# Hybrid streaming encoder step, `down` of the MLP: the order of two products, one tile pool for `up` and `down`, and the queue that loads x

## The chip, the cores and the metric

The kernel runs on one core of one Trainium2 chip. The time is that of one execution on the device, in microseconds (us); three runs of the kernel before the change took 2486.47, 2488.69 and 2491.09 us. A core has five engines that matter here: TensorE (PE in the profile; PEld is its weight load), VectorE (DVE), ScalarE (ACT), GpSimd (POOL) and SyncE (SP). Each runs its own instructions in order and waits for the others by semaphores. Transfers between DRAM and on-chip memory are issued by SP (the hardware queue q1 in the profile) and by POOL (the software queue q0), and both are served by the same 16 DMA engines.

## What is computed

One step of a two-layer encoder over T = 1024 + 64 frames of width 1024. Layer 0 mixes frames by windowed attention, layer 1 by a gated recurrence, and each layer ends in an MLP:

```python
def sqrelu_mlp(h, w_up, w_down):
    return jnp.square(jax.nn.relu(h @ w_up)) @ w_down
...
        yp = yp + sqrelu_mlp(rmsnorm(yp, mlp_norm[i]), mlp_w_up[i], mlp_w_down[i])
        ys = ys + sqrelu_mlp(rmsnorm(ys, mlp_norm[i]), mlp_w_up[i], mlp_w_down[i])
```

`w_up` is 1024 x 4096 and `w_down` 4096 x 1024, in fp32. The results are y of all frames, and the new caches and states of the mixers.

## The kernel before

**Numbers.** Every operand of TensorE is split into a rounded part and the rest (`hi` and `lo`, tiles `eh`/`el`, `xh`/`xl`, `whi`/`wlo`). A product then takes three matmuls: hi by hi, lo by hi, hi by lo. The rounding is a cast on ScalarE, the rest a subtraction on VectorE (lines 117 and 118 for weights, 998 and 999 for the operands of `down`).

**Products.** `up` and `down` each multiply a 2 x 2 block matrix by a 2 x 2 block matrix in seven products of sums of blocks. For `down` the table `PRODS` (from line 31) has a row for each: the weight blocks that are added or subtracted, the name of the operand, where the result is added in x, and the four slots that hold the operand. A slot is two tiles next to each other: `x2` is xh[2], xl[2], xh[3] and xl[3], so a product's operand has eight pieces of 128 x 1088.

**From `up` to `down`.** `up` runs over 16 pairs m of output blocks. At the end of each it holds four results (y) and forms five sums of them on VectorE (tiles `d1` or `d`, line 903). All are written to DRAM by POOL's queue (`keep`, line 840, tensor `y_mlp`), by the row of `PRODS` that uses them; piece k of an operand needs pairs 2k and 2k + 1. The last piece, number 7, needs the last pair. While `up` works x lies in DRAM (`x_mlp`), and its tiles `pair0` to `pair3` are `up`'s work space.

**`down`.** For product j, for each of four pairs m of output blocks, and for each slot i: `weights` loads a 256 KB block through SP's queue (line 1003, tile `raw`), loads a second one and adds or subtracts it where the row of `PRODS` has two (line 1010, tile `q`), and splits it; `mul` (line 1021) then issues 4 x 2 x 3 = 24 matmuls of 128 x 272. The result lies in one of four accumulators (`pu`), and `evacuate` (line 1030) adds it to x. As soon as an operand tile is read for the last time in product j, `load(j + 1, i)` (line 997) brings the next piece through POOL's queue. In product 0 the x tiles are loaded again, too (lines 1093 and 1095). At the end of layer 1 `normed` (line 1046) writes y.

**Tiles and their waits.** A tile comes from a pool. A pool that is opened after another was closed lies in the same memory, and its first tiles wait for all that the closed pool's tiles still do, their transfers included. Within a pool a tag has a fixed number of buffers, and a buffer is used again when its last reader is done. Before the change `up` has a pool `up` (tags `tt`, `d1`, `raw`, `q`) that closes before the pool `down` (`raw`, `q`, `y`) opens. The first weight block of a sum goes to a third pool that lives throughout (`raw`, three buffers); so do the split weights, two tiles of two halves each.

**What sets the order.** The program is written as above, but a scheduler orders each engine's instructions by a simulated time line, so instructions of `down` stand among the last of `up`.

Of the kernel before, what the change touches and what calls it, by code (L numbers as in the profile page):

```python
# [8 lines left out]
F32 = mybir.dt.float32  # L9
# [6 lines left out]
PSUM = bass.MemoryType.PSUM  # L16

P = 128
# [10 lines left out]


PRODS = (
# [18 lines left out]
class Trunk:  # L50
# [933 lines left out]
    def down(self, layer, final, hp, acc):  # L984
        nc, tc, A = self.nc, self.tc, self.A
        self.CH = CH4

        def pair_of(slot):
            i = int(slot[1])
            return [(self.eh, self.el) if slot[0] == "e" else (self.xh, self.xl)][0], (i, i + 1)  # L990


        def load(j, i):
            (hs, ls), n = pair_of(PRODS[j][3][i])
            for q, k in enumerate(n):
                y = ls[k][:].bitcast(F32)
                nc.gpsimd.dma_start(y, self.yk[layer][j, 2 * i + q].rearrange("p a n -> p (a n)"))
                nc.scalar.copy(hs[k][:], y)
                nc.vector.tensor_sub(ls[k][:], y, hs[k][:].bitcast(F32))

        def raw(m, block, i, own):
            r = self.raw() if own else hp.tile([P, 4, P], F32, name="raw", tag="raw", bufs=3)
            nc.sync.dma_start(r[:], A["w_down"][layer, 2 * m + block[0], :, block[1], 4 * i:4 * i + 4, :])
            return r[:]

        def weights(a, m, i):
            r = raw(m, a[0], i, True)
            if len(a) > 1:
                q = hp.tile([P, 4, P], F32, name="q", tag="q", bufs=2)[:]
                nc.vector.tensor_tensor(q, r, raw(m, a[2], i, False), ALU.add if a[1] == "+" else ALU.subtract)  # L1010
                r = q
            return self.parts(r)

        def mul(ps, w, j, i, cs, first, last):
            (hs, ls), n = pair_of(PRODS[j][3][i])
            for k in range(4):
                t, o = n[k // 2], TH * (k % 2)
                for c in cs:
                    s = slice(o + TH // 2 * c, o + TH // 2 * c + TH // 2)
                    for x, (a, b) in enumerate(((0, hs), (0, ls), (1, hs))):  # L1020
                        done = nc.tensor.matmul(ps[:, c, :], w[k][a], b[t][:, s], start=first and k == x == 0,  # L1021
                                                stop=last and k == 3 and x == 2)
            return done

        def evacuate(ps, m, outs, cs=(0, 1)):
            n = TH // 2
            for r, h, f in outs:
                for t, u in [(self.xp[m][:, r, TH * h:TH * h + TH].rearrange("p (c n) -> p c n", c=2), ps)] \
                        if len(cs) == 2 else [(self.xp[m][:, r, TH * h + n * c:TH * h + n * c + n], ps[:, c, :]) for c in cs]:
                    nc.vector.tensor_tensor(t, t, u, ALU.add if f == "+" else ALU.subtract)  # L1030

        def scale(k, cs):
            if not final:
                for c in cs:
                    self.scale_part(2, k, c)

        def square(k, cs):
            for c in cs:
                done = self.square_part(k, c)
            return done  # L1040

        def normed(c, ks):
            s, n = self.CH[c]
            for k in ks:
                y = hp.tile([P, 272], F32, name="y", tag="y", bufs=6)
                nc.vector.scalar_tensor_tensor(y[:, :n], self.x(k)[:, s:s + n], self.gains[:, 4, k:k + 1],
                                               self.rstd[:, s:s + n], ALU.mult, ALU.mult)
                nc.sync.dma_start(self.O["y"][:, k, s:s + n], y[:, :n])

        def norm(c):  # L1050
            self.norm_scale(c, acc()[:, 0, :])

        H0, H1 = (0, 1), (2, 3)
        self.xp = [None] * 4
        for i in range(4):
            load(0, i)
        done = None
        for j, (a, name, outs, slots) in enumerate(PRODS):
            end = j == len(PRODS) - 1
            for m in range(4):  # L1060
                order = list(range(4))
                if m == 3:
                    i = 3 if end else slots.index(PRODS[j + 1][3][3])
                    order = [i] + [k for k in order if k != i]
                ps = acc()
                if end and final and m == 3:
                    self.half = None
                    w = {i: weights(a, m, i) for i in order}
                    for c in range(2):
                        for i in order:  # L1070
                            mul(ps, w[i], j, i, (c,), i == order[0], i == order[-1])
                        evacuate(ps, m, outs, (c,))
                        done = square(7, (2 + c,))
                        if c == 0:
                            norm(2)
                            normed(2, range(3))
                    norm(3)
                    with tc.issue_after(done.ins):
                        normed(2, range(3, KT))
                        normed(3, range(KT))  # L1080
                    return
                for i in order:
                    last = mul(ps, weights(a, m, i), j, i, (0, 1), i == order[0], i == order[-1])
                    if end and m == 3 and i == order[0]:
                        for k in (0, 1):
                            scale(k, H0)
                        scale(0, H1)
                        scale(1, H1)
                if j == 0:
                    self.xp[m] = self.pair(m)  # L1090
                    if done:
                        with tc.issue_after(done.ins):
                            nc.sync.dma_start(self.xp[m][:], self.xk[layer][:, 2 * m:2 * m + 2, :])
                    else:
                        nc.sync.dma_start(self.xp[m][:], self.xk[layer][:, 2 * m:2 * m + 2, :])
                done = last
                evacuate(ps, m, outs)
                if not end and m < 3:
                    load(j + 1, m)

                if j == 5:
                    square(2 * m, H1)
                if end:
                    square(2 * m + 1, H1)
                    if m in (1, 2):
                        scale(2 * m + 1, H1)
                    if final and m < 2:
                        norm(m)
                        normed(m, range(KT))
            if not end:  # L1110
                load(j + 1, 3)
            if j == 4:
                self.new_norm()
                for k in range(KT):
                    square(k, H0)
            if j == 5:
                for k in range(2, KT):
                    scale(k, H0)
                for k in (2, 4, 6):
                    scale(k, H1)  # L1120
        scale(7, H1)

    def mlp(self, layer, wa, wb, na, final):
        tc = self.tc
        with ExitStack() as ctx:
            ep = ctx.enter_context(tc.tile_pool(name=f"mlp{layer}", bufs=1))
            with ExitStack() as c2:
                up = c2.enter_context(tc.tile_pool(name=f"up{layer}", bufs=1))
                with ExitStack() as c3:
                    self.banks(c3, f"mr{layer}", 8)  # L1130
                    op = self.operands(1 + 2 * layer, ep, up)
                    self.mix_rest(wa, wb, op, na)
                pu = ctx.enter_context(tc.tile_pool(name=f"pu{layer}", bufs=4, space=PSUM))

                def acc():
                    return pu.tile([P, 2, 512], F32, name="pu", tag="pu")[:, :, :TH // 2]

                self.up(layer, op, up, acc)
            with ExitStack() as c2:
                hp = c2.enter_context(tc.tile_pool(name=f"down{layer}", bufs=1))  # L1140
                self.down(layer, final, hp, acc)

    def run(self):
        A = self.A
# [131 lines left out]
```

## Time and profile before

| | |
|---|---|
| median of three runs | 2488.69 us |
| the profiled execution | 2486.93 us |
| its span, first to last instruction | 2485.2 us |
| mean granted TensorE clock | 0.984 of full speed |
| traffic of DRAM | 252.80 MB read, 81.79 MB written |
| hardware queue (SP) | 205.96 MB, 25.9% of the 16 engines' span |
| software queue (POOL) | 135.26 MB, 14.4% |

The profile is of one execution. An engine's busy time is the sum of its instructions; time in which it stands is put down to what released it. In layer 0 `up` ends and `down` begins at about 738 us of the span, in layer 1 at about 2099 us. A timeline row has the start, the length, the engine, the line, the operation and, in brackets, the idle time before it and its releaser. A row of waits has the engine and tile that waited, what for, the total, how often and the longest.

### The profile page before, as it was taken

Reading aid. Unit: us, or ns where it says so; the run is one execution under the profiler, and the core shown is the slowest. Engines: PE = TensorE matmul, PEld = TensorE weight load, DVE = VectorE, ACT = ScalarE, POOL = GpSimd, SP = SyncE. Lnnn points to the kernel's source line nnn. Section 1 sums busy time; section 2 is a strip of 40 time slices with the busy share of each in tenths; the row PEclk is TensorE's granted clock in tenths of the full one; section 3 lists DMA queues with packets and bytes.
Section 4 is the critical chain, followed back from the end, with each engine's and each line's share of the span. In section 5 each row is a group of like instructions: output and inputs, shape, how many; then the busy total and the mean of one; then the engine's idle time right before and its main releaser. Section 6 shows DMA issues by size and latency. Waiting matters only on the chain.

```text
span 2485.2 us, 46519 instructions
## 1 busy us (share of the span) xinstructions
PE 2389.9 (96%) x18474; PEld 2334.2 (94%) x18474; DVE 1747.8 (70%) x3120; ACT 1079.4 (43%) x2200; POOL 238.9 (10%) x481
## 2 busy tenths in 40 slices
PE   8999999999986999999999999999999997799997
PEld 7998899999986999999999999998999997799997
DVE  7555559877775577677677777776987777557766
ACT  5236546333342433445455555554633334243342
POOL 2211100111120100000000000000011113000000
PEclk9999999999998999999999999999999999899999
DMA  5322123443367687561111011023244446667764
GB/s 168 85 56 68 38 89 112 149 146 142 142 232 243 215 276 250 185 214 35 38 38 37 30 38 38 25 91 117 96 145 147 142 146 261 224 226 264 242 197 152
DMA packets 158922, 344.20 MB, mean 139 GB/s; under 512 B 35296, under 2 KB 47200, under 8 KB 154976
## 3 DMA queue, kind: packets, MB, share of 16 engines
q1 hardware_dynamic: 120784, 205.96, 25.9%
q0 software_dynamic: 37920, 135.26, 14.4%
q8 instruction: 146, 2.39, 0.4%
q14 instruction: 72, 0.59, 0.1%
HBM read 252.80 MB, written 81.79 MB: 135 GB/s over the span
## 4 chain that ended last, share of the span: by engine, by line
PE 73%; issue 17%; DMA 4%; POOL 3%; DVE 2%; ACT 1%; POOLq 0%; SPq 0%; DVEq 0%; ACTq 0%
PE pu L1021 18%; PE pu L891 13%; PE mm L127 10%; PE mm L129 9%; PE mm L128 9%; POOL y_mlp L840 2%; PE sc L341 2%; PE po L375 2%; PE pb L651 2%; PE pu L878 1%; DMA xl<-y_mlp 1%; DMA y_mlp<-d 1%; DMA raw<-in_w_down 1%; PE pb L615 1%; PE pt L369 1%
## 5 line engine op out<-in xcount | busy, mean ns | idle before, releaser
L127 PE MATMUL mm<-xh,whi 128*128 128x384 f32 (+2 forms) x1440 | 478.9, 333 | 13.9 <-ACT whi L117 11.7
L128 PE MATMUL mm<-xl,whi 128*128 128x384 f32 (+2 forms) x1440 | 474.7, 330 | 0.0
L129 PE MATMUL mm<-xh,wlo 128*128 128x384 f32 (+2 forms) x1440 | 473.5, 330 | 0.0
L1021 PE MATMUL pu<-xh,wlo 128*128 128x272 f32 x1024 | 296.4, 289 | 0.5 <-DVE wlo L118 0.3
L1021 PE MATMUL pu<-xh,whi 128*128 128x272 f32 x1024 | 296.0, 289 | 0.5 <-DVE pair L1030 0.5
L1021 PE MATMUL pu<-xl,whi 128*128 128x272 f32 x1024 | 295.7, 289 | 0.0
L127 PEld LDWEIGHTS mm<-xh,whi 128*128 128x128 f32 x1440 | 272.3, 189 | 19.7 <-ACT whi L117 12.8
L117 ACT CAST whi<-raw 128x512 fp32r<-128x512 f32 (+1 forms) x288 | 166.4, 608 | 261.6 <-PE mm L128 92.0
L1021 PE MATMUL pu<-eh,whi 128*128 128x272 f32 x768 | 224.3, 292 | 56.4 <-ACT whi L117 56.4
L891 PE MATMUL pu<-xh,wlo 128*128 128x272 f32 x960 | 276.6, 288 | 0.0
L128 PEld LDWEIGHTS mm<-xl,whi 128*128 128x128 f32 x1440 | 272.5, 189 | 3.5 <-issue 2.2
L891 PE MATMUL pu<-xl,whi 128*128 128x272 f32 x960 | 275.6, 287 | 0.0
L891 PE MATMUL pu<-xh,whi 128*128 128x272 f32 x960 | 275.4, 287 | 0.0
L129 PEld LDWEIGHTS mm<-xh,wlo 128*128 128x128 f32 x1440 | 272.2, 189 | 3.1 <-issue 1.2
L117 ACT CAST whi<-q 128x512 fp32r<-128x512 f32 x220 | 130.6, 618 | 279.7 <-PE pu L1021 187.6
L118 DVE TENSOR_TENSOR wlo<-raw,whi 128x512 fp32r<-128x512 f32 (+1 forms) x288 | 187.5, 673 | 62.4 <-ACT whi L117 61.9
L118 DVE TENSOR_TENSOR wlo<-q,whi 128x512 fp32r<-128x512 f32 x220 | 146.3, 687 | 112.1 <-ACT whi L117 111.5
L1021 PE MATMUL pu<-eh,wlo 128*128 128x272 f32 x768 | 224.0, 292 | 0.1
L1021 PE MATMUL pu<-el,whi 128*128 128x272 f32 x768 | 223.5, 291 | 0.0
L891 PE MATMUL pu<-eh,wlo 128*128 128x272 f32 x720 | 208.0, 289 | 0.0
L891 PE MATMUL pu<-eh,whi 128*128 128x272 f32 x720 | 207.5, 288 | 0.0
L891 PE MATMUL pu<-el,whi 128*128 128x272 f32 x720 | 207.0, 287 | 0.0
(281 smaller groups left out, 5529.0 us busy)
## 6 DMA issues: line engine op xcount, KB each, us to landing
raw<-in_w_down SPq DMA_DIRECT2D x384, 256.0 KB, 3.8
y_mlp<-d POOLq DMA_DIRECT2D x160, 272.0 KB, 2.5
xl<-y_mlp POOLq DMA_DIRECT2D x64, 544.0 KB, 8.0
raw<-in_w_up SPq DMA_DIRECT2D x128, 256.0 KB, 2.7
el<-y_mlp POOLq DMA_DIRECT2D x48, 544.0 KB, 6.9
y_mlp<-pair POOLq DMA_DIRECT2D x64, 272.0 KB, 2.4
raw<-in_w_in SPq DMA_DIRECT2D x64, 256.0 KB, 2.9
x_mlp<-pair SPq DMA_DIRECT2D x8, 1088.0 KB, 4.9
```

The lines of the kernel that those rows point to most:

```text
L117: nc.scalar.copy(hi, raw)
L118: nc.vector.tensor_sub(lo, raw, hi.bitcast(F32))
L127: nc.tensor.matmul(ps[:, :n], wh, ih[:, s:s + n], start=i == 0, stop=False)
L128: nc.tensor.matmul(ps[:, :n], wh, il[:, s:s + n], start=False, stop=False)
L129: nc.tensor.matmul(ps[:, :n], wl, ih[:, s:s + n], start=False, stop=i == last)
L341: nc.tensor.matmul(ps[u][:, i, :kn], st, kd[g][r, k0:k0 + kn], start=True, stop=True)
L369: nc.tensor.transpose(pt[:, kt, :], pb[:, u, kt * P:(kt + 1) * P], self.ident[:])
L375: nc.tensor.matmul(out, ptts[u][:, kt, :], v, start=start, stop=stop)
L651: nc.tensor.matmul(psa[r:r + 64 - hh, i // 2, :].rearrange("p (s t) -> p s t", t=hh), d[:, i * 64:i * 64 + 64 - hh], dv[:, i * ns:(i + 1) ...
L840: self.nc.gpsimd.dma_start(self.yk[layer][i, p // 2, :, p % 2, :], t)
L891: nc.tensor.matmul(ps[:, c, :], a, cols(b)[:, c, :], start=not more and p == i == 0, stop=p == 3 and i == 2, skip_group_check=True)
L1021: done = nc.tensor.matmul(ps[:, c, :], w[k][a], b[t][:, s], start=first and k == x == 0, stop=last and k == 3 and x == 2)
```

## The change

The first two rows of `PRODS` change places, but the slots stay with the place: product 0 is now the one of a single weight block, with the operand b21-b11, and product 1 the one of a sum, with b11. `up` and `down` share one pool, open from `up`'s start to `down`'s end; the second block of a sum has two buffers in it where it had three, and the y of the last norm is put into the tags `tt` and `d1`. The x tiles of product 0 are loaded through POOL's queue in place of SP's.

```diff
--- before.py
+++ after.py
@@ -29,8 +29,8 @@
 
 
 PRODS = (
-    (((1, 0), "+", (1, 1)), "b11", ((1, 0, "+"), (1, 1, "-")), ("e0", "e2", "x0", "x2")),
-    (((1, 1),), "b21-b11", ((1, 0, "+"), (0, 0, "+")), ("e4", "x4", "x6", "x0")),
+    (((1, 1),), "b21-b11", ((1, 0, "+"), (0, 0, "+")), ("e0", "e2", "x0", "x2")),
+    (((1, 0), "+", (1, 1)), "b11", ((1, 0, "+"), (1, 1, "-")), ("e4", "x4", "x6", "x0")),
     (((0, 1), "-", (1, 1)), "b21+b22", ((0, 0, "+"),), ("e0", "e2", "x2", "x4")),
     (((0, 0), "+", (0, 1)), "b22", ((0, 0, "-"), (0, 1, "+")), ("e4", "x0", "x6", "x2")),
     (((0, 0), "+", (1, 1)), "b11+b22", ((0, 0, "+"), (1, 1, "+")), ("e0", "e2", "x4", "e4")),
@@ -999,7 +999,7 @@
                 nc.vector.tensor_sub(ls[k][:], y, hs[k][:].bitcast(F32))
 
         def raw(m, block, i, own):
-            r = self.raw() if own else hp.tile([P, 4, P], F32, name="raw", tag="raw", bufs=3)
+            r = self.raw() if own else hp.tile([P, 4, P], F32, name="raw", tag="raw", bufs=2)
             nc.sync.dma_start(r[:], A["w_down"][layer, 2 * m + block[0], :, block[1], 4 * i:4 * i + 4, :])
             return r[:]
 
@@ -1042,7 +1042,7 @@
         def normed(c, ks):
             s, n = self.CH[c]
             for k in ks:
-                y = hp.tile([P, 272], F32, name="y", tag="y", bufs=6)
+                y = hp.tile([P, TH], F32, name="y", tag=("tt", "d1")[k % 2], bufs=3 + k % 2)
                 nc.vector.scalar_tensor_tensor(y[:, :n], self.x(k)[:, s:s + n], self.gains[:, 4, k:k + 1],
                                                self.rstd[:, s:s + n], ALU.mult, ALU.mult)
                 nc.sync.dma_start(self.O["y"][:, k, s:s + n], y[:, :n])
@@ -1090,9 +1090,9 @@
                     self.xp[m] = self.pair(m)
                     if done:
                         with tc.issue_after(done.ins):
-                            nc.sync.dma_start(self.xp[m][:], self.xk[layer][:, 2 * m:2 * m + 2, :])
+                            nc.gpsimd.dma_start(self.xp[m][:], self.xk[layer][:, 2 * m:2 * m + 2, :])
                     else:
-                        nc.sync.dma_start(self.xp[m][:], self.xk[layer][:, 2 * m:2 * m + 2, :])
+                        nc.gpsimd.dma_start(self.xp[m][:], self.xk[layer][:, 2 * m:2 * m + 2, :])
                 done = last
                 evacuate(ps, m, outs)
                 if not end and m < 3:
@@ -1124,21 +1124,18 @@
         tc = self.tc
         with ExitStack() as ctx:
             ep = ctx.enter_context(tc.tile_pool(name=f"mlp{layer}", bufs=1))
+            up = ctx.enter_context(tc.tile_pool(name=f"up{layer}", bufs=1))
             with ExitStack() as c2:
-                up = c2.enter_context(tc.tile_pool(name=f"up{layer}", bufs=1))
-                with ExitStack() as c3:
-                    self.banks(c3, f"mr{layer}", 8)
-                    op = self.operands(1 + 2 * layer, ep, up)
-                    self.mix_rest(wa, wb, op, na)
-                pu = ctx.enter_context(tc.tile_pool(name=f"pu{layer}", bufs=4, space=PSUM))
-
-                def acc():
-                    return pu.tile([P, 2, 512], F32, name="pu", tag="pu")[:, :, :TH // 2]
-
-                self.up(layer, op, up, acc)
-            with ExitStack() as c2:
-                hp = c2.enter_context(tc.tile_pool(name=f"down{layer}", bufs=1))
-                self.down(layer, final, hp, acc)
+                self.banks(c2, f"mr{layer}", 8)
+                op = self.operands(1 + 2 * layer, ep, up)
+                self.mix_rest(wa, wb, op, na)
+            pu = ctx.enter_context(tc.tile_pool(name=f"pu{layer}", bufs=4, space=PSUM))
+
+            def acc():
+                return pu.tile([P, 2, 512], F32, name="pu", tag="pu")[:, :, :TH // 2]
+
+            self.up(layer, op, up, acc)
+            self.down(layer, final, up, acc)
 
     def run(self):
         A = self.A
```

**SP's queue at the change of stages (layer 0).** Before; `in_w_up` and `in_w_down` are the weights in DRAM, `pair` the x tiles; `DMAHW`, `DMASW` stand for transfers of SP's and POOL's queue that must have ended:

```order
L1003 DMA raw_8272<-in_w_down 128x512 [waits DMAHW0_49,DVE_49]
L883 DMA raw_8101<-in_w_up 128x512 [waits DMAHW6_49,DVE_49]
L1003 DMA raw_8306<-in_w_down 128x512 [waits DMAHW5_49,DVE_49]
L1095 DMA pair0_8372<-x_mlp0 128x2176 [waits DMASW3_49,DMASW4_49,DVE_49,Activation_49]
L1093 DMA pair2_8658<-x_mlp0 128x2176 [waits DVE_49]
L1093 DMA pair3_8801<-x_mlp0 128x2176 [waits DVE_49]
L1093 DMA pair1_8515<-x_mlp0 128x2176 [waits DMASW3_49,DMASW1_49,DMAHW1_49,DVE_49,Activation_49]
L1003 DMA raw_8243<-in_w_down 128x512 [waits DMASW6_49,DMASW5_49,DMASW7_49,DMASW4_49,DMAHW2_49,DMASW3_49,DMAHW4_49,DMASW2_49,DMASW0_49]
L1003 DMA raw_8275<-in_w_down 128x512 [waits DMAHW3_49]
```

With the change:

```order
L1003 DMA raw_8264<-in_w_down 128x512 [waits DMAHW0_49,DVE_49]
L883 DMA raw_8101<-in_w_up 128x512 [waits DMAHW6_49,DVE_49]
L1003 DMA raw_8294<-in_w_down 128x512 [waits DMAHW5_49,DVE_49]
L1003 DMA raw_8747<-in_w_down 128x512 [waits DMAHW4_49,DVE_49]
L1003 DMA raw_8779<-in_w_down 128x512 [waits DMAHW2_49,DVE_49]
L1003 DMA raw_8322<-in_w_down 128x512 [waits DMAHW1_49,DVE_49]
L1003 DMA raw_8363<-in_w_down 128x512 [waits DMAHW3_49,DVE_49]
L1003 DMA raw_8391<-in_w_down 128x512 [waits DMAHW5_49,DVE_49]
L1003 DMA raw_8421<-in_w_down 128x512 [waits DMAHW0_49,DVE_49]
L1003 DMA raw_8449<-in_w_down 128x512 [waits DMAHW1_49,DVE_49]
```

The x tiles are gone from SP, and so is the block that waits for nine transfers (the first tile of the pool `down`). Two second blocks of product 1 (raw_8747, raw_8779) stand ahead of product 0's fourth block, and each block waits for VectorE's last reading of its buffer alone.

**POOL's queue, the last y pieces (layer 0).** Before; `d1` are `up`'s sums, `xl3` the last piece of product 0's operand; the last two sums follow behind:

```order
L840 DMA y_mlp0<-d1_8134 128x544 [waits DMASW4_49,DVE_49]
L997 DMA el5_3759<-y_mlp0 128x1088 [waits DMASW5_49,PE_49]
L997 DMA xl4_74<-y_mlp0 128x1088 [waits DMASW6_49,PE_49]
L997 DMA xl5_75<-y_mlp0 128x1088 [waits DMASW7_49,PE_49]
L997 DMA xl6_76<-y_mlp0 128x1088 [waits DMASW0_49,PE_49]
L997 DMA xl7_77<-y_mlp0 128x1088 [waits DMASW1_49,PE_49]
L840 DMA y_mlp0<-d1_8166 128x544 [waits DMASW2_49,DVE_49]
L840 DMA y_mlp0<-d1_8169 128x544 [waits DMASW3_49,DVE_49]
L997 DMA xl3_73<-y_mlp0 128x1088 [waits DMASW4_49]
```

With the change:

```order
L840 DMA y_mlp0<-d1_8134 128x544 [waits DMASW7_49,DVE_49]
L997 DMA xl5_75<-y_mlp0 128x1088 [waits DMASW0_49,PE_49]
L997 DMA xl6_76<-y_mlp0 128x1088 [waits DMASW1_49,PE_49]
L997 DMA xl7_77<-y_mlp0 128x1088 [waits DMASW2_49,PE_49]
L1093 DMA pair2_8606<-x_mlp0 128x2176 [waits DMAHW4_49,DMAHW6_49,DMASW3_49,DVE_49]
L1093 DMA pair3_8733<-x_mlp0 128x2176 [waits DMAHW1_49,DMAHW7_49,DMASW4_49,DVE_49]
L840 DMA y_mlp0<-d1_8166 128x544 [waits DMASW5_49,DVE_49]
L840 DMA y_mlp0<-d1_8169 128x544 [waits DMASW6_49,DVE_49]
L840 DMA y_mlp0<-d1_8205 128x544 [waits DMASW7_49,DVE_49]
L840 DMA y_mlp0<-d1_8208 128x544 [waits DMASW0_49,DVE_49]
L1093 DMA pair1_8479<-x_mlp0 128x2176 [waits DMAHW5_49,DMASW1_49,Activation_49]
L997 DMA xl3_73<-y_mlp0 128x1088 [waits DMASW5_49,DMASW2_49]
```

Three x tiles stand in this queue now (the fourth, pair0, is nine places ahead of the first row), two of them ahead of the last four sums and all ahead of xl3, which waits for two transfers of its own queue.

**TensorE, product 0 (layer 0).** Before, behind the first half of the last slot (xh2) comes its second half (xh3):

```order
L1021 MATMUL pu_8239<-xh2_64,whi_8344 128x272
L1021 MATMUL pu_8239<-xl2_72,whi_8344 128x272
L1021 MATMUL pu_8239<-xh2_64,wlo_8345 128x272
L1021 MATMUL pu_8239<-xh3_65,whi_8344 128x272
L1021 MATMUL pu_8239<-xl3_73,whi_8344 128x272
L1021 MATMUL pu_8239<-xh3_65,wlo_8345 128x272
```

With the change the next m comes there:

```order
L1021 MATMUL pu_8235<-xh2_64,whi_8324 128x272
L1021 MATMUL pu_8235<-xl2_72,whi_8324 128x272
L1021 MATMUL pu_8235<-xh2_64,wlo_8325 128x272
L1021 MATMUL pu_8362<-eh0_3748,whi_8324 128x272 [waits PE_49,Activation_49]
L1021 MATMUL pu_8362<-el0_3754,whi_8324 128x272
L1021 MATMUL pu_8362<-eh0_3748,wlo_8325 128x272 [waits DVE_49]
```

Further on, the fourth block of that m is begun with `whi` alone, then matmuls of the m behind it, then `wlo`:

```order
L1021 MATMUL pu_8362<-xh1_63,wlo_8394 128x272
L1021 MATMUL pu_8362<-xh2_64,whi_8451 128x272 [waits Activation_49]
L1021 MATMUL pu_8362<-xl2_72,whi_8451 128x272
L1021 MATMUL pu_8489<-eh0_3748,whi_8451 128x272 [waits PE_49,Activation_49]
L1021 MATMUL pu_8489<-el0_3754,whi_8451 128x272
L1021 MATMUL pu_8362<-xh2_64,wlo_8452 128x272 [waits DVE_49]
```

And here the first matmul on xh3 stands, for two accumulators in turn:

```order
L1021 MATMUL pu_8489<-eh1_3749,wlo_8452 128x272
L1021 MATMUL pu_8235<-xh3_65,whi_8324 128x272 [waits Activation_49]
L1021 MATMUL pu_8362<-xh3_65,whi_8451 128x272
L1021 MATMUL pu_8235<-xl3_73,whi_8324 128x272 [waits DVE_49]
L1021 MATMUL pu_8235<-xh3_65,wlo_8325 128x272
L1021 MATMUL pu_8235<-xh3_65,whi_8324 128x272
```

The first matmul of `down` is row 4705 of TensorE's order in both kernels. The first on xh3 is row 4789 before and row 4897 with the change: 84 matmuls of `down` stand ahead of it there, and 192 here. Layer 1 has the same pattern.

## The prediction

> **What bounds the kernel now.** I read the page's busy shares first, then TensorE's waits, then the one place they name: by stretches, by the transfer queue's waits, by the chain and by the transfers.
>
> ```profile
> PE 2389.9 (96%) x18474; PEld 2334.2 (94%) x18474; DVE 1747.8 (70%) x3120; ACT 1079.4 (43%) x2200; POOL 238.9 (10%) x481
> PE pu L1021 <- ACT whi L117: 56.4, 2, 28.3
> PE mm L127 <- ACT whi L117: 11.7, 1, 11.7
> PE pb L753 <- ACT hon L752: 3.6, 5, 1.5
> ```
>
> TensorE is busy for 96%, so only its gaps can be won. Two gaps hold 56.4 us: line 1021 is the product of `down`, it waits once in each layer, and what it waits for is the cast of a weight block. The next gap, at the program's start, is untouched by the change, and the others are small.
>
> ```profile
> 700.00:738.40 38.40, 0.00 (x0) 0.00 (x0) 1.00 0.65 234
> 738.40:766.40 28.00, 0.00 (x0) 0.00 (x0) 0.58 0.86 345
> 766.40:806.40 40.00, 39.85 (x301) 39.53 (x302) 0.95 0.65 203
> 806.40:846.40 40.00, 40.00 (x320) 40.00 (x319) 1.00 0.57 193
> 2098.90:2127.20 28.30, 0.01 (x1) 0.01 (x1) 0.55 0.86 342
> 2127.20:2167.20 40.00, 40.00 (x298) 39.78 (x299) 0.94 0.64 200
> ```
>
> These are stretches, counting line 1021 alone: length, matmuls in brackets, granted clock, transfer share, GB/s. A full stretch of 40 us holds 320 matmuls, 0.125 us each. The one behind the gap holds 301, and 298 in layer 1, at a clock of 0.95 and 0.94: another 19 and 22 matmuls, 2.4 and 2.8 us, go with the gap. **What the gaps cost in all:** 56.4 + 5.2 = 61.6 us.
>
> ```profile
> SPq L1093 <- DVE pair L909: 17.1, 1, 17.1
> SPq L1003 <- DMA y_mlp<-d: 14.2, 1, 14.2
> 749.30 12.47 DMA y_mlp<-d
> 762.42 3.58 DMA raw<-in_w_down
> ```
>
> The first two rows are what SP's transfer queue waited for around the first gap, the others the chain of waits there. SP first stands for the x tiles (their place still serves `up`), then line 1003, the second weight block of a sum, stands 14.2 us for the writes of `up`'s last sums to DRAM: its tile belongs to a pool laid over `up`'s. The last write lands at 761.8, the block 3.6 us later, then come the sum and the cast, and TensorE starts at 766.5.
>
> ```profile
> DMA packets 3315, 14.80 MB, mean 361 GB/s; under 512 B 432, under 2 KB 432, under 8 KB 2800
> GB/s 438 413 418 408 393 417 408 428 413 418 437 418 443 403 428 408 438 393 428 423 428 403 423 398 413 423 418 343 104 50 0 0 213 220 356 110 164 229 344 396
> 730.26 0.53 POOL L997 DMA_DIRECT2D xl<-y_mlp  x1 [5.40 <-PE pu L891]
> 736.80 1.11 ACT L998 CAST xh<-xl 128x1088 fp32r<-128x1088 f32 x1 [0.99 <-PE pu L891]
> 757.77 1.10 ACT L998 CAST xh<-xl 128x1088 fp32r<-128x1088 f32 x1 [0.20 <-DMA xl<-y_mlp]
> 760.39 1.10 ACT L998 CAST xh<-xl 128x1088 fp32r<-128x1088 f32 x1 [1.52 <-DMA xl<-y_mlp]
> 761.52 1.29 DVE L999 TENSOR_TENSOR xl<-xl,xh 128x1088 fp32r<-128x1088 f32 x1 [1.32 <-ACT xh L998]
> ```
>
> The first row is the traffic of 721 to 762, the second its rate in 40 slices of 735 to 770: the engines run full at some 413 GB/s until 759. So the gap hides a **transfer backlog**: 14.8 MB of y, x and sums. The last piece of product 0's operand, xl3 (the 760.39 row), comes 22 us after `up`'s end at 738.4. Taking away the weights' wait does not take away this one.
>
> **The change part by part.**
>
> *One pool, product 0 with single blocks.* The first weights now want neither a sum nor a tile of another pool. The order on SP in the change has no wait for nine transfers left, and the first three blocks are asked for before `up` ends, as they were. Pieces xl0 to xl2 were there in time already (cast from 736.80; product 0 reaches x0 48 matmuls in, at 744.4). So TensorE runs on at 738.4. Removed: 61.6 us. The weight sums of product 0 move to product 1; seven products with five sums stay, so the number of casts, sums and blocks doesn't change. What is late next is xl3.
>
> *How far TensorE gets.* Its order in the change has 192 matmuls of `down` before the first on xh3: 192 x 0.125 = 24.0 us, to 762.4. Just ahead stands a weight tile whose place comes free only with the matmuls before it, so a cast and a subtraction stand bare:
>
> ```profile
> 765.79 0.62 ACT L117 CAST whi<-q 128x512 fp32r<-128x512 f32 x1 [4.31 <-DVE q L1010]
> 770.39 0.69 DVE L118 TENSOR_TENSOR wlo<-q,whi 128x512 fp32r<-128x512 f32 x1
> ```
>
> 0.62 + 0.69, with the semaphores some 1.5 us: TensorE is at xh3 at 763.9.
>
> *When xl3 comes.* x now goes through POOL's queue, and xl3 stands behind all four x tiles and all sums there.
>
> ```profile
> pair<-x_mlp SPq DMA_DIRECT2D x3, 1088.0 KB, 9.5
> xl<-y_mlp POOLq DMA_DIRECT2D x64, 544.0 KB, 8.0
> y_mlp<-d POOLq DMA_DIRECT2D x160, 272.0 KB, 2.5
> raw<-in_w_down SPq DMA_DIRECT2D x384, 256.0 KB, 3.8
> ```
>
> From the first load of `down` to xl3 that queue carries 14 pieces of 544 KB, 9 sums and results of 272 KB and 4 x tiles of 1088 KB: 14,416 KB, 14.76 MB, which is the 14.80 MB that ended at 761.8. What is new beside it are weights, which SP no longer holds back: two blocks for product 1, and six for product 0 while TensorE runs, 8 x 256 KB = 2.1 MB, 5.1 us at 413 GB/s. So I let xl3 land at 761.8 + 5.1 = 766.9, and its cast (1.10) and subtraction (1.29) end at 769.3. The wait behind xh3 is then 769.3 - 763.9 = 5.4, and with the 1.5 the new gaps are 6.9 us. Bounds: xl3 in time costs nothing but the 1.5; if the one queue moved its bytes 10 us slower, it would be 16.9. I take 6.9, the full rate, since a saturated stretch with the same bytes is the nearest row.
>
> *The clock behind the new gap.* The gap of 28 us cost 2.4 to 2.8; in two stretches of `up`'s start TensorE stood idle for 0.9 of 5 us each (its busy time comes first, the other engines' behind) and kept its clock of 1.00:
>
> ```profile
> 345.00:350.00 5.00, 4.06 (x30) 3.69 (x29) 1.91 (x4) 1.75 (x5) 0.00 (x0) 1.00 0.06 14
> 350.00:355.00 5.00, 4.09 (x24) 3.77 (x25) 2.00 (x5) 1.64 (x6) 0.00 (x0) 1.00 0.48 146
> ```
>
> A gap of 5.4 lies between; I take 1.5 of 0 to 2.6. [...] That the clock falls behind a long gap the stretches above show; at which length it falls, none does.
>
> *Two buffers in place of three for a sum's second block.* Priced at nothing: in the two-block products TensorE never waits for weights in the trace, with landings of 3.8 us (median) against 2 x 24 x 0.125 = 6.0 us for two blocks' use. What hides it are the two sums and four weight halves made ahead. Where this cover goes is a rival below.
>
> *The final y in tiles of `up`, SP's shorter queue at the start.* A slot is used again after six y or more, as before; nothing within a few tenths of a us either way, because y leaves from the same queue at the same distance.
>
> **Sum.** Against the profiled execution (2486.9 us, span 2485.2): 61.6 removed, 2 x (6.9 + 1.5) = 16.8 added, 44.8 less: 2442.1. The median of the three runs lies 1.8 above the profiled one, which would make it 2443.9. I predict 2443.
>
> **The rivals.**
>
> *A: the last piece hides.* In the one queue the y pieces pass ahead of x, which before took about half the rate beside them (three tiles of 1088 KB at 9.5 us each, overlapping); xl3 could be cast by 764. Then only the 1.5 remain: 61.6 - 3.0 = 58.6 less, 2428. Against it: x is ahead of xl3 itself, and the bytes are the same.
>
> *B: POOL's queue holds more up than its bytes.* POOL waits in order. Two x loads now stand ahead of the sums, and each waits for VectorE's last use of its place: SP's rows above had 17.1 us for the first, to 740.4. Sums, and so xl3, come later, and ScalarE's casts of xh4 to xh7 stand ahead of weight casts in its order. With 10 us more in each layer: 61.6 - 2 x 18.4 = 24.8 less, 2462.
>
> ```profile
> L997 POOL DMA_DIRECT2D xl<-y_mlp x64: 530/530/547, 730.3 to 2412.4; - x64
> ```
>
> An issue on POOL takes 530 to 547 ns whatever VectorE does, so the issuing itself does not stretch. [...]
>
> *C, slower: the weight feed in two-block products.* While the next operand loads, blocks land late:
>
> ```profile
> DMA to landing us min/median/max: 4.1/8.2/9.9
> ```
>
> That is line 1003 in 855 to 875 us. With two buffers one block then comes every (8.2 + 0.33 issue + 0.69 sum) / 2 = 4.6 us against 3.0 used. In 20 us 4.3 come and 6.7 go: 2.4 blocks, 7 us, short. Four to six made ahead cover this; if nothing did, ten such bursts in two layers cost 70 us, 25 more than the gain: 2512. It decides from 4.5 us a burst. Against it: TensorE's list of waits has no such wait now, even with these landings.
>
> *D: nothing is won.* If the pool's wait stayed, or x0 to x2 came as late as xl3, TensorE would stand until 760 as it does: 2487. The order on SP speaks against the first, the 736.80 row against the second.
>
> **How the numbers follow.** Forecast (2432 to 2454) 0.66, A 0.13, B 0.13, C 0.04, D 0.04. The range takes in A and B to their ends, 2427 to 2463. Faster by over 0.2% (5 us, about what a measurement of this kernel can tell from no change): 0.66 + 0.13 + 0.13 = 0.92; same 0.04 from D; slower 0.04 from C.
>
> **What would show it.** Right: TensorE has no gap at the end of `up`; a gap of about 1.5 and one of 3 to 8 us some 24 us later, the second released by ScalarE's cast of xh3, itself released by xl3; the transfers full until 767; some 310 or more matmuls in the 40 us behind it. Wrong: a gap at 738 (A weight not there), a cast of xh3 before 764 (A), one after 772 with SP or POOL standing (B), waits for weights in products 1 to 4 and 6 (C).

## The result, and the profile after

| | before | after |
|---|---|---|
| median | 2488.21 us (2486.47 to 2491.09, 4 runs) | 2446.46 us (2444.47 to 2448.89, 4 runs) |
| ratio, 95% interval | 1 | 0.9832 (0.9814 to 0.9849) |
| the profiled execution | 2486.93 us | 2448.89 us |
| its span | 2485.2 us | 2447.1 us |
| mean granted clock | 0.984 | 0.992 |

The change takes 41.8 us off the median. The busy times, from the page after the change:

```profile
PE 2395.6 (98%) x18474; PEld 2338.2 (96%) x18474; DVE 1746.3 (71%) x3120; ACT 1079.8 (44%) x2200; POOL 243.0 (10%) x489
```

TensorE's waits at line 1021, from the view of waits after (what for: total, how often, longest):

```profile
PE pu L1021 <- ACT xh L998: 7.3, 2, 3.8
PE pu L1021 <- ACT whi L117: 3.0, 4, 1.0
PE pu L1021 <- DVE wlo L118: 1.9, 3, 0.9
PE pu L1021 <- DVE xl L999: 1.4, 2, 0.8
```

The 56.4 us of before are gone. In their place stand 13.6 us in short waits, and what is waited for most is no longer a weight but the operand piece xh3. The timeline shows where, in layer 0. TensorE's last row of `up` is at 743.11 in this execution (in the attention stage 10.2 us, 236.5 to 246.7, and 3.4 us, 355.9 to 359.3, ran at half clock in this execution, against 3.4 us before, 285.7 to 289.1, so all stands 5.1 us later than in the profile before):

```profile
743.23 0.29 PE L1021 MATMUL pu<-eh,whi 128*128 128x272 f32 x1
760.93 0.40 PE L1021 MATMUL pu<-xh,whi 128*128 128x272 f32 x1 [0.89 <-ACT whi L117]
762.34 0.40 PE L1021 MATMUL pu<-xh,wlo 128*128 128x272 f32 x1 [0.89 <-DVE wlo L118]
765.96 0.39 PE L1021 MATMUL pu<-xh,whi 128*128 128x272 f32 x1 [0.58 <-ACT whi L117]
774.57 0.52 PE L1021 MATMUL pu<-xh,whi 128*128 128x272 f32 x2 [3.52 <-ACT xh L998]
775.89 0.59 PE L1021 MATMUL pu<-xl,whi 128*128 128x272 f32 x1 [0.81 <-DVE xl L999]
```

The first matmul of `down` follows `up` without a gap. Three short waits for a weight (0.89 + 0.89 + 0.58 = 2.4 us) come 17 to 22 us on, and at xh3 TensorE stands for 3.52 + 0.81 = 4.3 us. What xh3 waits for stands on POOL and ScalarE (timeline, same execution):

```profile
756.46 0.54 POOL L840 DMA_DIRECT2D y_mlp<-d  x1 [1.41 <-DMA xl<-y_mlp]
757.82 0.54 POOL L1093 DMA_DIRECT2D pair<-x_mlp  x1 [0.81 <-ACT xh L998]
766.65 0.54 POOL L997 DMA_DIRECT2D xl<-y_mlp  x1 [8.29 <-DMA y_mlp<-d]
773.42 1.10 ACT L998 CAST xh<-xl 128x1088 fp32r<-128x1088 f32 x1 [6.99 <-DMA xl<-y_mlp]
```

The last sum is issued at 756.46; POOL then stands 8.29 us until it has landed, issues xl3, and the cast can begin 6.8 us after that, 30.0 us behind `up`'s end (743.11 + 0.29). The traffic of 730 to 790, in 40 slices of 1.5 us, has the engines full until 772:

```profile
GB/s 279 284 392 394 445 399 413 419 405 424 418 407 413 413 420 402 406 422 423 409 406 409 414 401 439 399 405 354 82 0 11 0 0 0 123 227 169 157 23 113
```

Behind the waits, line 1021 alone in stretches of 40 us (length, TensorE's and its weight loads' busy time with their counts, granted clock, transfer share, GB/s), layer 0 and layer 1:

```profile
776.00:816.00 40.00, 39.84 (x303) 39.62 (x304) 0.96 0.67 237
2115.00:2155.00 40.00, 40.00 (x297) 40.00 (x298) 0.93 0.65 230
```

303 and 297 matmuls, where a full stretch has 320: 17 and 23 are missing, 2.1 and 2.9 us. That is about as much as the gap of 28 us had left behind it (19 and 22): here waits of 4.3 and 4.4 us at xh3 cost the clock about what those of 28 had. The clock in steps of 1 us, layer 0, shows how (these rows count all engines; the granted clock is third from the end):

```profile
775.00:776.00 1.00, 0.19 (x2) 0.11 (x1) 0.84 (x1) 0.00 (x0) 0.00 (x0) 0.88 0.05 16
776.00:777.00 1.00, 1.00 (x5) 1.00 (x6) 0.00 (x0) 0.00 (x0) 0.00 (x0) 0.50 0.00 0
779.00:780.00 1.00, 1.00 (x9) 1.00 (x9) 1.00 (x2) 0.70 (x2) 0.00 (x0) 0.91 0.00 0
```

It is half, not a little lower, and only from 775.8 to 779.2: 3.4 us at half clock, 1.7 us lost. In layer 1 it is half from 2113.8 to 2120.6, 6.8 us, and 3.4 us are lost. Behind the gaps of before TensorE ran at half clock for 3.9 and 5.1 us (to 770.4 and 2132.3).

**Where the time went.** From `up`'s last matmul to `down`'s last, layer 0 took 738.05 to 1108.00 before and takes 743.11 to 1092.25 now, 20.8 us less; layer 1 2098.62 to 2471.54 and 2081.73 to 2434.09, 20.6 less. The 41.4 are the change; the 5.1 us of the attention stage, and 1.8 won between the layers and at the end, make up the 38.1 by which the two spans differ.

### The profile page after: what moved, and what is told of

Read it like the earlier page. It is cut to its first block, busy times and chain, and to the rows that moved or that the text cites. A ratio compares the mean times of both kernels' runs of the same rounds, so it can differ in the third digit from the quotient of the medians.

```text
span 2447.1 us, 46493 instructions
## 1 busy us (share of the span) xinstructions
PE 2395.6 (98%) x18474; PEld 2338.2 (96%) x18474; DVE 1746.3 (71%) x3120; ACT 1079.8 (44%) x2200; POOL 243.0 (10%) x489
## 4 chain that ended last, share of the span: by engine, by line
PE 76%; issue 15%; POOL 3%; DMA 3%; DVE 2%; ACT 1%; POOLq 0%; SPq 0%; DVEq 0%; ACTq 0%
PE pu L1021 26%; PE mm L127 10%; PE mm L128 10%; PE mm L129 10%; PE pu L891 8%; POOL y_mlp L840 3%; PE sc L341 2%; PE po L375 2%; PE pb L651 2%; PE pu L878 1%; DMA xl<-y_mlp 1%; PE pt L369 1%; PE pb L615 1%; DMA el<-y_mlp 1%; PE pb L738 1%
## 5 line engine op out<-in xcount | busy, mean ns | idle before, releaser
L1021 PE MATMUL pu<-xh,whi 128*128 128x272 f32 x1024 | 297.8, 291 | 10.8 <-ACT xh L998 7.3
L1021 PEld LDWEIGHTS pu<-xh,whi 128*128 128x128 f32 x1024 | 194.3, 190 | 12.4 <-ACT xh L998 7.7
```

## The experiments

Theory: the gap of before was a weight wait with a backlog of transfers under it. Three edits took part: the swap, the common pool, the queue. Rivals: one of the three does it all; or xl3 is late by POOL's order and not by bytes. Each kernel is compared with the kernel before, run beside it on the same chip.

| | swap | one pool | x through | median us | ratio (95%) |
|---|---|---|---|---|---|
| r1, r5: the change again | yes | yes | POOL | 2444.58, 2444.91 | 0.9825 (0.981 to 0.9839), 0.983 (0.9817 to 0.9844) |
| r2 | yes | no | SP | 2451.81 | 0.9849 (0.9835 to 0.9864) |
| r3 | no | yes | SP | 2458.97 | 0.9878 (0.9862 to 0.9895) |
| r4 | yes | yes | SP | 2452.75 | 0.9851 (0.9836 to 0.9866) |
| r7 | no | yes | POOL | 2450.95 | 0.9854 (0.984 to 0.9867) |
| r8 | no | no | POOL | 2480.99 | 0.9972 (0.9962 to 0.9983) |
| r6, r10 | yes | yes | POOL, behind xl3 | 2430.03, 2431.19 | 0.9767 (0.9754 to 0.9781), 0.9773 (0.9755 to 0.9791) |
| r9 | no | yes | POOL, behind xl3 | 2451.34 | 0.9849 (0.9832 to 0.9865) |

### The change again (r1, r5)

> The changed kernel again, to be compared with the next three on the same chip. Expected: 0.982 to 0.985 of the kernel before (2446 of 2488). In the profile no gap of TensorE where `up` ends, two to three gaps of under 1 us for weight casts and one of 3 to 6 us at xh3 in each layer.

> The changed kernel again, beside the others of this set: 2443 to 2449 us, with gaps of 6 to 8 us in each layer at the start of down, the longest released by the cast of xh3.

Both times came out as expected. The waits of a layer do not repeat as closely: 7.0 and 4.4 us in r1, 4.7 and 7.3 in r5, because the wait at xh3 before its cast is 3.8 to 4.1 us in one layer and 1.5 in the other, not always the same one. So one layer of each run lies below what was expected of its gaps.

### The swap alone (r2)

```diff
 PRODS = (
-    (((1, 0), "+", (1, 1)), "b11", ..., ("e0", "e2", "x0", "x2")),
-    (((1, 1),), "b21-b11", ..., ("e4", "x4", "x6", "x0")),
+    (((1, 1),), "b21-b11", ..., ("e0", "e2", "x0", "x2")),
+    (((1, 0), "+", (1, 1)), "b11", ..., ("e4", "x4", "x6", "x0")),
```

> Only the two rows of PRODS change places; pools and x's queue are those of the kernel before. Theory 1 (the gap was the wait for the second blocks' tile; once it is gone the transfer backlog sets the restart at xh3, whoever carries x): single blocks need no tile of the pool of `down`, so TensorE runs on at the end of `up`; at xh3 it waits 3 to 6 us, and since SP now stands at the first second block (of product 1) until the last sums have landed, the weights of the third m come some 3 us later still. Sum of gaps 6 to 11 us a layer, 2446 to 2456 us. Rival (it takes the shared pool, too): the gap stays at 20 us or more in each layer, 2475 to 2488 us.

2451.81 is within the theory's range: 36 us of the 43 come from one edit of two rows. The waits at the start of `down`, 8.0 and 8.6 us in the two layers, are within its range, too, but none of them is at xh3, where it put 3 to 6 us. The longest, one in each layer, are for a weight cast; r4 shows what holds it up:

```profile
762.86 0.59 PE L1021 MATMUL pu<-xh,whi 128*128 128x272 f32 x1 [6.09 <-ACT whi L117]
2107.09 0.59 PE L1021 MATMUL pu<-xh,whi 128*128 128x272 f32 x1 [7.14 <-ACT whi L117]
```

### The common pool alone (r3)

```diff
-            with ExitStack() as c2:
-                up = c2.enter_context(tc.tile_pool(name=f"up{layer}", bufs=1))
+            up = ctx.enter_context(tc.tile_pool(name=f"up{layer}", bufs=1))
...
-                hp = c2.enter_context(tc.tile_pool(name=f"down{layer}", bufs=1))
-                self.down(layer, final, hp, acc)
+            self.down(layer, final, up, acc)
```

> Only the shared pool (with its two buffers and the y tags); product 0 keeps the sums of two blocks, x stays on SP. Theory 1: no wait for the sums' landing at the first block, so TensorE runs on at the end of `up`; but its order reaches xh3 after 108 matmuls, 13.5 us, and b11's last piece lands no earlier than 20 us behind the end of `up`, so it waits there for some 8 to 10 us and the clock falls: 10 to 13 us a layer, 2448 to 2454 us. Rival (the single blocks are what counts, a sum needs SP's second block behind the x loads): gaps of 15 us or more, 2460 to 2480 us.

2458.97 lies between the two ranges. The pool alone takes the 28 us wait away, too, as the theory said; so either edit does it, and their gains (36 and 29 us) do not add. But the theory had the wrong wait behind it. At xh3, where it put 8 to 10 us, TensorE waits for 0.9 us in layer 0 and 1.9 in layer 1. What it waits for are two-block weights, 8.9 and 8.8 us, which the rival named with 15 us or more. In layer 0 the longest are:

```profile
749.35 0.48 PE L1021 MATMUL pu<-xh,wlo 128*128 128x272 f32 x1 [3.74 <-DVE wlo L118]
759.02 0.39 PE L1021 MATMUL pu<-eh,whi 128*128 128x272 f32 x1 [3.60 <-ACT whi L117]
```

### x through SP (r4)

```diff
-                            nc.gpsimd.dma_start(self.xp[m][:], self.xk[layer][:, 2 * m:2 * m + 2, :])
+                            nc.sync.dma_start(self.xp[m][:], self.xk[layer][:, 2 * m:2 * m + 2, :])
```

(and the line without `done` alike)

> The change without its queue: swap and shared pool, but x loaded through SP as before. Theory 1 (the bytes ahead of xl3 count, not their queue): within 4 us of the changed kernel, xh3 cast 28 to 31 us behind the end of `up`. Rival (POOL's queue, waiting in order, is what makes xl3 late): xh3 cast 5 us or more earlier, 8 us or more faster than the changed kernel. Other rival (SP's weights stand behind x again): gaps of more than 3 us for weights, slower than the changed kernel by 6 us or more.

The theory missed: xh3 is cast 33.7 us behind `up`'s end, and the time is not within 4 us. The last of the three came true, 8.2 us slower than r1, but by another way than it said: the weight is not late, its cast is. TensorE's wait in layer 0, and ScalarE's rows around it:

```profile
765.05 0.59 PE L1021 MATMUL pu<-xh,whi 128*128 128x272 f32 x1 [9.61 <-ACT whi L117]
761.37 1.10 ACT L998 CAST xh<-xl 128x1088 fp32r<-128x1088 f32 x1 [2.87 <-DMA xl<-y_mlp]
763.38 1.10 ACT L998 CAST xh<-xl 128x1088 fp32r<-128x1088 f32 x1 [0.92 <-DMA xl<-y_mlp]
764.39 0.61 ACT L117 CAST whi<-raw 128x512 fp32r<-128x512 f32 x1
772.52 1.10 ACT L998 CAST xh<-xl 128x1088 fp32r<-128x1088 f32 x1
```

In these rows ScalarE casts in program order, and the casts of product 1's operand (xh4 to xh7) stand ahead of `whi`. They wait for their y pieces, the last two for 2.87 and 0.92 us, and these share the transfer engines with x on SP's queue. With x on POOL's queue y passes ahead: in r1 the last of the same four casts begins at 754.10 and `whi` at 755.11. There xl3 is what comes late (cast at 768.51, waited for), while here it is cast right behind the next weights, at 772.52, and not waited for. So the queue trades a wait of 9.6 us for one of 2 to 5. Issuing x takes 0.53 us on POOL and 0.33 on SP, and the rate is about 410 GB/s either way (some 413 in the profile before, with x on SP, and 408 to 420 in that of the change, with x on POOL), yet the queue is worth 8.2 us here: it decides which bytes go first.

### Without the swap (r7), and the queue alone (r8)

r7 is the change with the two rows of `PRODS` in their old order. r8 is the kernel before, with both x loads on `nc.gpsimd`.

> The change without the swap: one pool and x on POOL's queue, but product 0 has the sums of weight blocks again. Theory: y passes ahead of x, so ScalarE's casts of xh4 to xh7 come early and do not hold the weight casts, but each piece of product 0 needs two blocks through full transfer engines: gaps of 3 to 4 us for the cast or the subtraction of a weight, once or twice in each layer, and xl3's wait partly behind them: 8 to 12 us of gaps in each layer, 2449 to 2457. Rival: with x out of SP's way two blocks come as easily as one, gaps as in the changed kernel, within 3 us of it (the swap is worth nothing).

> The third part of the change alone: x through POOL's queue; products, pools and weight sums as before. Theory: the wait of 28 us is for the release of up's pool, which comes when up's last sums have landed, and these land as late as before (23.2 us behind up's end in the changed kernel, 23.4 in the kernel before), so the gap stays at 26 to 30 us in each layer and the time within 4 us of the kernel before. Rival: x out of SP's way lets the first weight blocks come sooner; the gap falls to 20 us or less, 2470 or below.

r7 has 2450.95, within the theory's range, with waits of 7.6 and 7.2 us in the two layers, a little under the 8 expected. The longest, in its timeline, is for a weight of two blocks:

```profile
761.77 0.39 PE L1021 MATMUL pu<-eh,whi 128*128 128x272 f32 x1 [2.53 <-ACT whi L117]
```

The swap is worth 6.0 us here and 6.2 with x on SP (r3 against r4).

r8 gains 7.0 us, more than the 4 expected. The gaps stay, as the theory says:

```profile
765.04 0.59 PE L1021 MATMUL pu<-eh,whi 128*128 128x272 f32 x1 [26.04 <-ACT whi L117]
2123.47 0.59 PE L1021 MATMUL pu<-eh,whi 128*128 128x272 f32 x1 [27.01 <-ACT whi L117]
```

They are 3.4 us shorter than before, and from `up`'s last matmul to `down`'s last the two layers are 4.7 us shorter; where the rest lies was not followed.

### x behind xl3 (r6, r10)

`load` returns its transfer, and the x loads are ordered behind the last of them on POOL:

```diff
-                nc.gpsimd.dma_start(y, self.yk[layer][j, 2 * i + q].rearrange("p a n -> p (a n)"))
+                got = nc.gpsimd.dma_start(y, self.yk[layer][j, 2 * i + q].rearrange("p a n -> p (a n)"))
...
+            return got
...
-            load(0, i)
+            got = load(0, i)
...
-                    if done:
-                        with tc.issue_after(done.ins):
-                            nc.gpsimd.dma_start(self.xp[m][:], self.xk[layer][:, 2 * m:2 * m + 2, :])
-                    else:
+                    with tc.issue_after(got.ins):
                         nc.gpsimd.dma_start(self.xp[m][:], self.xk[layer][:, 2 * m:2 * m + 2, :])
```

> The change, but the four x tiles stand behind xl3 in POOL's queue instead of ahead of it. Theory: xl3 is late because 4.46 MB of x pass ahead of it through full transfer engines (10.8 us at 413 GB/s); with x behind it, its cast ends before TensorE reaches xh3, the gap of 3.5 to 3.8 us and the slow clock behind it go, and only the weight gaps (2.4 us in each layer) remain: 4 to 5 us in each layer less than the changed kernel, 8 to 11 in all, about 2435. Rival: xl3 is late because POOL stands for the landing of up's last sums whatever lies ahead; then the cast comes no more than 2 us earlier and the time stays within 3 us of the changed kernel. Other rival: x now comes too late for the first additions to x, the accumulators stay taken, and TensorE waits for VectorE in product 1: 5 us or more slower than the changed kernel.

> x behind xl3 with the swap, again, beside the one without: 2428 to 2431 us, gaps of 1.8 to 1.9 us in each layer, all of them for weights.

The theory's direction, and more than its size: r6 takes 14.9 us less than r5, beside it on the same chip, and r10 repeats it (2431.19). TensorE's waits in layer 0, and POOL's and ScalarE's rows of xl3 (TensorE's first matmul of `down` is at 737.89 here; the edit moves line 1021 to 1022):

```profile
756.09 0.39 PE L1022 MATMUL pu<-xh,wlo 128*128 128x272 f32 x1 [0.83 <-DVE wlo L118]
759.71 0.39 PE L1022 MATMUL pu<-xh,whi 128*128 128x272 f32 x1 [0.58 <-ACT whi L117]
768.47 0.39 PE L1022 MATMUL pu<-eh,wlo 128*128 128x272 f32 x1 [0.41 <-DVE wlo L118]
750.89 1.17 POOL L840 DMA_DIRECT2D y_mlp<-d  x2 [5.54 <-DVE d L903]
753.27 0.54 POOL L997 DMA_DIRECT2D xl<-y_mlp  x1 [1.22 <-DMA y_mlp<-d]
753.80 2.11 POOL L1093 DMA_DIRECT2D pair<-x_mlp  x4
760.09 1.10 ACT L998 CAST xh<-xl 128x1088 fp32r<-128x1088 f32 x1
```

POOL stands 1.22 us for the last sum where it stood 8.29, so the long wait was the sum's own way through the backlog of x, not the order alone. The cast of xl3 comes 22.2 us after `down`'s first matmul, 30.2 in the changed kernel, and nothing waits for it. By the bytes alone (the estimate of the expectation) it would have been 10.8 us earlier; it is 8.0. Nor does anything wait for x. The waits fall from 4.7 and 7.3 us (r5, layers 0 and 1) to 1.8 and 1.9, which is 8.2 in all; `down` is 6.1 and 9.1 us shorter from its first matmul to its last, 15.2, so the matmuls themselves run 7 us faster. The clock accounts for it: in r5 it is half for 6.8 us in each layer's `down` (757.9 to 761.3 and 771.6 to 775.0 in layer 0, a mean of 0.83 over 2105 to 2125 in layer 1), which loses 6.8 us in all, and in r6 it is 1.00 in all stretches of 735 to 1085 and of 2065 to 2178. **This kernel is faster than both**, by 57 us against before.

### x behind xl3 without the swap (r9)

The edit of r6 on r7.

> One pool, x behind xl3 in POOL's queue, but the sums of weight blocks first (no swap). Theory: with single blocks first the swap took 6 us off in both queue orders (2450.95 against 2444.9, 2458.97 against 2452.75), by the weight blocks that two-block pieces want from full transfer engines; these engines are still full here, so 4 to 8 us slower than x behind xl3 with the swap: 2434 to 2438, with gaps of 5 to 8 us in each layer for weights. Rival: the 4.46 MB of x that no longer stand ahead leave room for the second blocks; within 2 us of it, and the swap is worth nothing there.

Neither came true: 2451.34 is 20 us slower than r10 beside it. The waits are those expected (7.5 and 6.9 us in the two layers), the time is not. The longest wait in its timeline:

```profile
754.58 0.59 PE L1022 MATMUL pu<-xh,wlo 128*128 128x272 f32 x1 [5.12 <-DVE wlo L118]
```

And line 1022 in the stretches behind it:

```profile
755.00:760.00 5.00, 4.42 (x26) 4.12 (x26) 0.75 1.03 426
760.00:765.00 5.00, 3.46 (x23) 3.01 (x23) 0.93 1.02 417
765.00:770.00 5.00, 5.00 (x32) 5.00 (x32) 0.73 1.03 419
```

A stretch of 5 us holds some 42 matmuls at full clock (775 to 780 in this profile, at 1.00); here two of three have a mean clock of three quarters. So the waits cost clock as well. `down` is 9.4 us longer than r10's in layer 0 and 9.1 in layer 1. All its waits together are 10.6 us longer than r10's, and the clock is half for 6.8 us in layer 0 (by the mean clocks of 750 to 770) and, by the matmuls 0.23 us apart, for 8.3 in layer 1 (2097.3 to 2105.6), where r10's matmuls stay 0.125 us apart: up to another 7.5 us. The expectation did not count the clock. x behind xl3 is worth 15 us with the swap (r6 against r5) and nothing without it (ratios of 0.9849 in r9 and 0.9854 in r7): then the weights are what comes late.

## Why the prediction was right

The forecast was 2443 us (2427 to 2463); the median is 2446.46.

- *What is removed, 61.6 us.* The two gaps of 56.4 went, in the way named: no gap at `up`'s end, and no weight waits for a pool. But the swap and the pool each do it (r2, r3), which the prediction took as one edit.
- *What is late next.* xl3, as it said, through the backlog. Its landing was put 28.5 us behind `up`; it came 30.0 (773.42 less 743.4). The transfers were to be full until then, and were until 28.6. r6 shows that the bytes of x ahead of it are the cause. That POOL would stand for the sum's landing belonged to rival B; it did, for 8.29 us, but as a part of the same backlog, not beside it.
- *The new gaps, 6.9 us a layer.* Measured 6.85 and 6.80. The two parts are off against each other: 2.4 for weights where 1.5 was taken (three waits, not two), and 4.3 at xh3 where 5.4 was taken. That their sum fits to 0.1 us is luck. TensorE reached xh3 27.7 us behind `up`'s end instead of 25.5, and could go on behind the subtraction at 32.5 instead of 30.9; between stand two matmuls that need xh3 alone.
- *The clock, 1.5 us a layer.* This is the term that was mis-sized. It cost 2.1 and 2.9 us by the missing matmuls, 1.7 and 3.4 by the half clock. With the former the sum is 61.6 - 13.7 - 5.0 = 42.9 less, against 41.4 measured in `down` (the 1.5 us between them were not followed); the forecast had 44.8. "Some 310 or more matmuls" in the 40 us behind did not come: 303 and 297. The row that spoke for a small price, 345 to 355 us at a clock of 1.00, was misread and lucky. It lies at the end of the attention stage; `up`'s first matmuls (line 878) start at 396.4. And in the profile of the change the same place, 3.5 us later, has 3.4 us at half clock (355 to 360 us are at 0.66, behind waits of 0.52, 0.52, 0.38 and 0.42 us; the profile before has 0.52, 0.52, 0.39 and 0.42 there, at 1.00). Layer 0 had 3.4 us at half clock behind a wait of 3.5; layer 1 paid twice that behind one of 3.8.
- *At nothing: two buffers, the tiles of y.* TensorE has no wait for weights in products 1 to 6, so C has no place; nothing in the waits comes from y.
- *The rivals.* A (xl3 hides) is what r6 makes true by another order. B has its mechanism on both sides: ScalarE's casts of xh4 to xh7 hold a weight cast up in r2 and r4, where x is on SP, and POOL's queue cures that. It was put down to the wrong queue. D did not come.
- *That issuing on POOL does not stretch.* POOL's issues at lines 840, 997, 1093 and 1095 take 0.53 to 0.56 us after, where those at 840 and 997 took 0.53 to 0.56 before, with four x loads a layer among them now and VectorE busy for 71%: no issue took longer.

## What to carry to other kernels

Where an engine waits for a weight at the change of stages, look under the wait for a transfer backlog, and order the transfers by who needs them first: bytes that are wanted last (here x) behind the ones that are wanted next, in the same queue (14.9 us here, r6 against r5). The choice of a queue was here a choice of that order, and of what stands behind a waiting instruction (8.2 us, r4 against r1). Two such edits can be worth little singly and much together: the swap took 6 us off with x ahead and 20 with x behind, and the waits of some 4 us in the changed kernel's two layers cost 1.7 and 3.4 us at half clock besides.

## What was not expected of the hardware

In these profiles the granted clock also fell behind shorter waits, and not each time. In r5, layer 0, two waits of 0.88 and 0.90 us with two matmuls between them were followed by a slow stretch. From its timeline (rows behind the second wait are 0.23 us apart, where 0.125 is usual):

```profile
756.53 0.39 PE L1021 MATMUL pu<-xh,whi 128*128 128x272 f32 x1 [0.88 <-ACT whi L117]
757.95 0.60 PE L1021 MATMUL pu<-xh,wlo 128*128 128x272 f32 x1 [0.90 <-DVE wlo L118]
758.79 0.43 PE L1021 MATMUL pu<-xh,wlo 128*128 128x272 f32 x1
759.02 0.43 PE L1021 MATMUL pu<-xh,whi 128*128 128x272 f32 x1
```

And line 1021 in stretches, in the same execution: the second stretch lies behind its wait of 1.48 + 0.81 us at xh3.

```profile
755.00:760.00 5.00, 3.22 (x17) 2.78 (x16) 0.79 1.01 409
770.00:775.00 5.00, 4.19 (x21) 4.07 (x21) 0.66 0.02 3
```

In the profiled execution of the change the same pair of waits (0.89 and 0.89) left the clock at 1.00. So in r5 idle times of 2.3 and of 1.8 us, each with two matmuls in it, were followed by half clock; in the profile of the change 1.8 us with two matmuls in it were not.

From 755 to 785 us the mean clock of 1 us steps is 1.00 or 0.50 in r5 and in the profile of the change, but for the steps in which a slow stretch begins or ends. In r5 the two stretches run from 757.9 to 761.3 and from 771.6 to 775.0, 3.4 us each. In the profile of the change they last 3.4 us in layer 0 and 6.8 in layer 1, and in the profile before 27.3 us (743.1 to 770.4) and 30.7 (2101.6 to 2132.3), most of it within the gaps. Why the same pair of waits cost 1.7 us of clock in r5 and nothing in the profile of the change is not shown.
